# First layer's output product: two of four column chunks as groups of seven products of sums

## The chip, the cores and the metric

The kernel runs on one core of one Trainium2 chip. TensorE (PE) multiplies matrices, VectorE (DVE) and ScalarE (ACT) and GpSimd (POOL) work elementwise, SyncE (SP) issues most transfers. The time is device microseconds of one execution, the median of several. Engines run their own instruction queues in order and wait for one another by semaphores.

## The reference, cut to what matters

Two layers of a gated block over 16 meta tokens and 512 tokens (T = 528), width 1024, float32. What the change touches is the last line of the layer:

```python
def hybrid_layer(x, norm_g, w_in, qn_g, kn_g, pool_w, pool_b, pool_s, w_a, w_b, w_out, cos, sin, k_top):
    h = rms_norm(x, norm_g)
    proj = jnp.einsum('btd,de->bte', h, w_in)
    ...
    g_a, g_b = jnp.split(jax.nn.sigmoid(merge), 2, axis=-1)
    return x + jnp.einsum('btd,de->bte', g_a * y_a + g_b * y_b, w_out)
```

The second layer begins with the norm of this sum and its product with `w_in`.

## The kernel before

**Layout.** Activations stand with features on the partitions: `RES[0]` (the residual, 8 tiles of 128 features by 528 tokens), `hhi` and `hlo`. A float32 operand is split in a high part (a cast to a shorter format, on ACT) and a low part (what the cast left, by a subtraction on DVE or POOL); a product is then high x high + high x low + low x high, three matmuls for each 128 features. Tokens come in two halves, columns 0 to 272 and 272 to 528 (`halves`).

**Weights.** `chunks` (L116 to L135) lists column chunks of the weights in order of use: 256 columns of all 1024 rows of `w_out` make one. `w_load` (L158) fetches a chunk into two of four `raw` tiles (512 KB each) when the tiles of the chunk two before are free. `w_prep_enqueue` (L176) puts the steps that split it into the queue `prep_q`; `group_done` (L367) takes one step after each matmul group. There are three ways to split, each filling `w` tiles, of which there are eight:

- plain: two casts on ACT, two subtractions of 128x1024 on DVE (`high`, `low`), four `w` tiles.
- `by_dma`: ACT writes the negated high part into the low tile, then a transfer that POOL issues adds the raw weights to it in place (`minus`, L218), and ACT casts the high part (`plus`, L223). After `plus(1)` the raw tiles are given back once that transfer has landed, and POOL starts the first sum of the chunk behind (`first_sum`, L253).
- `mixed`: the four 512x128 blocks of a chunk become seven operands, each high and low: a12, a11, s2, s1, s3, s4, a22 (`mixed_prep`, L257, steps `i0` to `i8`). The sums s3 and s4 are made by transfers issued by POOL that add in place: `first_sum` (raw<-raw, L255) and raw<-s (L284); s2 and s1 by DVE. Each operand takes one `w` tile.

**Products of sums.** `group_of_products` (L992) multiplies a `mixed` chunk by seven sums of activations, in three PSUM banks U, S, X, with 12 matmuls a product in place of the eight blockwise products (Winograd's form): a11, a12, s2, s1, s3, s4, a22. Between products that add to one bank, ACT copies the bank out (`p1`, `u2`, `p5`), and DVE adds these parts (`total`) and hands the result on (`direct`). `prep_one` calls in it keep the split of the chunk behind going by a count (`base`, `LEAD`). Layer 0 uses it for the merging gates with 264 columns, layer 1 also for the last two chunks of its output (`mix_out`, L1146) with the sums of `sums_of_merged` (L1085) on 256 columns: `first` and `sums` make a0-a1, b1-a1 and -b1-a0, `lows` their low parts, `fourth`, `last_high`, `last_low` the fourth sum.

**Layer 0's output before.** All four chunks are plain. `out_group` (L1438) calls `dense` (L588): 24 matmuls into one bank, then DVE adds half of the bank to `RES[0]`, ACT squares the result, POOL adds the squares into `sq` (L1448). Chunks 0 and 1 run half by half; then chunks 2 and 3 are both ready and all of the first half runs before the second (loop at L1476), so that `stats(0)` (mean squares by one-column matmuls, then POOL's power) and `norm_half(1, 0, ...)` (scale by token, L503) of the first half run beside the four groups of the second half. Layer 1 begins with `plain_trio` (L571), which reads `nf`, the scaled first half, and raw weights for keys.

**Order of work.** PE's and DVE's queues are in the order written (`manual_schedule`); ACT's, POOL's and SP's are put in order when the program is built. `later(fn, n)` runs a step n groups later.

## Time and profile before

| | |
|---|---|
| median of three runs | 741.03 us (740.54 to 742.34) |
| the profiled execution | 740.78 us |
| its span, first to last instruction | 738.8 us |
| PE busy | 731.2 us (99%), 5949 matmuls |
| DVE busy | 590.0 us (80%) |
| ACT busy | 483.1 us (65%) |
| POOL busy | 246.1 us (33%) |
| layer 0's output product, first matmul to layer 1's first | 332.36 to 381.11 us |
| layer 1's groups of seven on its output | 709.6 to 731.6 us |

Rows in order of time read: start in us, length in us, engine, line, operation, tile written <- tiles read, sizes, count, and in brackets the idle time before and what ended it. A row "x3" is three instructions merged. Nearly all PE and DVE rows have line L63, the helper that records them, so they are told apart by tiles: `d` is a bank of a dense group, `a` a bank of small products, `w` split weights, `raw` fetched weights, `osum` the sums of the merged activations, `res` the residual, `sqs` the summed squares, `msq` the mean squares, `nf` the normed activations, `c`, `p`, `u` the parts inside a group of seven. In the stretches the number after each busy time is the count of instructions. DMA rows give the size and the median time from issue to landing.

### The profile page before, as it was taken

What the parts mean: (1) busy time and instruction counts of PE and PEld (TensorE: products, weight loads), DVE (VectorE), ACT (ScalarE), POOL (GpSimd) and SP (SyncE); (2) the same over time, 40 slices, a digit from 0 to 9 for tenths busy, and PEclk for the clock granted to TensorE, in tenths of its full rate; (3) what the DMA queues carried; (4) which work ended last, traced back from release to release, by engine and by line L of the source; (5) the groups of instructions that cost most, each with busy time, mean ns of one, the idle gap of its engine ahead of it and who ended that gap; (6) DMA issues with size and microseconds to landing.
All of it is one profiled execution on the core that took longest, in us unless ns stands there. A gap on an engine that the chain in (4) does not pass through costs nothing.

```text
span 738.8 us, 16099 instructions
## 1 busy us (share of the span) xinstructions
PE 731.2 (99%) x5949; PEld 705.3 (95%) x5949; DVE 590.0 (80%) x1500; ACT 483.1 (65%) x1099; POOL 246.1 (33%) x320
## 2 busy tenths in 40 slices
PE   8999999999999999999999999999999999999998
PEld 7999998899999999999999989998899999999997
DVE  6866999999997775894349668999989978768874
ACT  6769735656788886643245696367488978775643
POOL 3742173721222211163347421756031321106300
PEclk9999999999999999999999999999999999999999
DMA  8766765864564434543422678659565553439932
GB/s 266 232 171 157 165 153 115 217 157 101 134 126 114 93 81 114 173 160 116 144 89 86 171 170 201 158 125 204 114 148 110 142 115 89 116 104 266 203 88 72
DMA packets 103566, 106.41 MB, mean 144 GB/s; under 512 B 5008, under 2 KB 83632, under 8 KB 103488
## 3 DMA queue, kind: packets, MB, share of 16 engines
q1 hardware_dynamic: 91888, 74.89, 33.8%
q0 software_dynamic: 11520, 30.41, 22.9%
q8 instruction: 46, 0.75, 0.4%
q14 instruction: 32, 0.26, 0.1%
q10 hardware_dynamic: 80, 0.08, 0.1%
HBM read 66.41 MB, written 8.55 MB: 101 GB/s over the span
## 4 chain that ended last, share of the span: by engine, by line
PE 75%; DVE 17%; ACT 2%; DMA 2%; issue 2%; POOL 1%; SPq 1%; DVEq 0%; POOLq 0%; ACTq 0%
PE d L63 60%; PE a L63 10%; DVE sc L63 5%; PE v L63 4%; DVE m L63 3%; DMA xt<-in_x_dram 2%; DVE t L63 1%; DVE w L63 1%; DVE nf L63 1%; DVE silb L63 1%; DVE us L63 1%; DVE mlo L63 1%; DMA raw<-s 1%; ACT w L225 0%; SPq L156 0%
## 5 line engine op out<-in xcount | busy, mean ns | idle before, releaser
L63 PE MATMUL d<-hhi,w 128*128 128x256 f32 (+3 forms) x1392 | 278.4, 291 | 0.1
L63 PEld LDWEIGHTS d<-hhi,w 128*128 128x128 f32 x1392 | 222.2, 188 | 3.2 <-issue 0.6
L63 PE MATMUL d<-hlo,w 128*128 128x256 f32 (+3 forms) x696 | 189.8, 289 | 0.0
L63 PEld LDWEIGHTS d<-hlo,w 128*128 128x128 f32 x696 | 131.3, 189 | 1.4 <-issue 0.2
L63 DVE TENSOR_TENSOR w<-raw,w 128x512 fp32r<-128x512 f32 (+1 forms) x156 | 121.4, 784 | 13.3 <-ACT w L269 12.9
L63 PE MATMUL d<-hsum,w 128*128 128x264 f32 (+1 forms) x720 | 95.4, 285 | 0.1
L63 PEld LDWEIGHTS d<-hsum,w 128*128 128x128 f32 x720 | 89.5, 188 | 0.8 <-issue 0.3
L63 PE MATMUL d<-w,hhi 128*128 128x256 f32 x576 | 86.2, 287 | 0.7 <-ACT sq L668 0.7
L269 ACT CAST w<-raw 128x512 fp32r<-128x512 f32 x132 | 79.1, 623 | 5.6 <-DMA raw<-s 4.2
L63 PEld LDWEIGHTS d<-w,hhi 128*128 128x128 f32 x576 | 74.7, 188 | 5.2 <-issue 2.3
L255 POOL DMA_DIRECT2D raw<-raw x22 | 19.9, 903 | 114.2 <-DVE w L63 36.7
L221 POOL DMA_DIRECT2D w<-raw x34 | 31.5, 943 | 73.7 <-ACT w L220 51.1
L63 DVE MATCH_REPLACE8 sc<-m,sc 128x400 f32<-128x400 f32 (+2 forms) x100 | 54.3, 547 | 0.0
L63 DVE MAX8 m<-sc 128x8 f32<-128x400 f32 (+2 forms) x100 | 53.1, 555 | 0.9
L791 ACT ACTIVATE lt<-lt,mn,NR 128x144 f32<-128x144 f32 (+3 forms) x64 | 42.2, 661 | 12.1 <-DVE mn L63 12.0
L284 POOL DMA_DIRECT2D raw<-s x22 | 19.6, 892 | 90.6 <-DVE s L63 42.8
L63 DVE SCALAR_TENSOR_TENSOR sc<-r,wsg,sc 128x144 f32<-128x144 f32 (+3 forms) x56 | 32.4, 581 | 17.4 <-ACT r L714 15.0
L63 PE MATMUL d<-w,hlo 128*128 128x256 f32 x288 | 45.5, 281 | 0.0
L63 PE MATMUL d<-mhi,w 128*128 128x272 f32 (+2 forms) x192 | 45.3, 324 | 0.0
L806 POOL TENSOR_SCALAR pm<-lt,rs 128x16 f32<-128x16 f32 x48 | 27.9, 622 | 44.7 <-DVE rs L63 31.9
L677 POOL TENSOR_TENSOR t<-t,t 128x256 f32<-128x256 f32 (+1 forms) x34 | 32.5, 956 | 26.4 <-DVE t L63 25.0
L1420 POOL TENSOR_TENSOR hlo<-ta,hhi 128x256 fp32r<-128x256 f32 (+1 forms) x28 | 26.8, 968 | 41.5 <-PE d L63 29.4
(245 smaller groups left out, 1559.1 us busy)
## 6 DMA issues: line engine op xcount, KB each, us to landing
raw<-in_w_in_dram SPq DMA_DIRECT2D x88, 256.0 KB, 3.4
w<-raw POOLq DMA_DIRECT2D x34, 512.0 KB, 5.9
raw<-in_w_in_dram SPq DMA_DIRECT2D x32, 512.0 KB, 4.4
raw<-in_w_out_dram SPq DMA_DIRECT2D x12, 512.0 KB, 4.6
raw<-raw POOLq DMA_DIRECT2D x22, 256.0 KB, 4.0
raw<-s POOLq DMA_DIRECT2D x22, 256.0 KB, 3.7
kept<-res SPq DMA_DIRECT2D x16, 264.0 KB, 4.6
res<-kept SPq DMA_DIRECT2D x16, 264.0 KB, 6.3
```

Source lines behind the costliest of these rows:

```text
L63: return fn(*a, **k)
L221: gp.dma_start(t, raws[c][s], accum_op=OP.add)
L255: gp.dma_start(raws[c][0][:, 1], raws[c][0][:, 0], accum_op=OP.add)
L269: act.copy(t[:, 0], blk[src[n]])
L284: gp.dma_start(blk["a12"], blk["s2"], accum_op=OP.add)
L677: added[0] = gp.tensor_tensor(t1[:m, :256], t1[:m, :256], t2[:m, :256], op=OP.add).ins
L791: act.activation(L[hh][:, :n], L[hh][:, :n], AF.Exp, scale=NR[:, i, h:h + 1], bias=mn[:, hh:hh + 1], accum_out=sm[:, hh:hh + 1])
L806: (gp if j < 3 else dve).tensor_scalar(pms[i][:, 2 * j + hh, :], L[hh][:, 0:16], rs[:, hh:hh + 1], None, op0=OP.mult)
L1420: pool_end = gp.tensor_sub(hlo[:, j, a:a + n], d, f(hhi[:, j, a:a + n]))
```

## The change

Layer 0's output uses chunks 0, 1 (first token half), 2, 3, 1 again (second half) in this order. Chunks 0 and 1 are split `by_dma`, chunk 1 is fetched and split twice; chunks 2 and 3 are `mixed` and run as two groups of seven products on 264 columns. `sums_of_merged` takes the start and width of the halves; its sums lie in other tiles when the width is 264, and the low parts of the fourth sum go to POOL. They are made during chunks 0 and 1. `stats(0)` follows the first group of the last chunk; `norm_half(1, 0, ...)` is called in the middle of the last group, by the new argument `mid` of `dense`. The square sums of the first half need no separate last tile any more, which halves the matmuls of `stats(0)`. `more` in `group_of_products` takes up to four preparing steps earlier in the second group. `tight` names the mixed chunks that split a12 before a11.

```diff
         chunks += [[(w_rows(w_a[l], c, 512), 0)] for c in (0, 512)]
-        chunks += [[(w_rows(w_out[l], c, 256), 0)] for c in (0, 256, 512, 768)]
+        if l == 0:
+
+            by_dma |= {len(chunks), len(chunks) + 1, len(chunks) + 4}
+            mixed |= {len(chunks) + 2, len(chunks) + 3}
+            tight = {len(chunks) + 3}
+        chunks += [[(w_rows(w_out[l], c, 256), 0)] for c in (0, 256, 512, 768) + ((256,) if l == 0 else ())]
...
-        soon = c <= len(chunks) - 2
+        soon = c not in tight
...
-    def dense(w, mt_, a, n, rhs=H, kt=KT, late=False):
+    def dense(w, mt_, a, n, rhs=H, kt=KT, late=False, mid=None):
...
+            if mid and e + 1 == len(steps) // 2:
+                mid()
...
-            while prep_q and (popped[0] < base + 9 * r + LEAD + done[0] * 9 // 7 or (mid and done[0] > 4)):
+            while prep_q and (popped[0] < base + 9 * r + LEAD + done[0] * 9 // 7 + min(more * done[0], 4) or (mid and done[0] > 4)):
...
-    def sums_of_merged(ta):
+    def sums_of_merged(ta, s0, n2, lag):
 
-        c0, c1 = slice(16, 272), slice(272, 528)
-        t1 = one.tile([128, 2, 4, 256], F32R, tag="D", name="osum1")
+        c0, c1 = slice(s0, s0 + n2), slice(s0 + n2, s0 + 2 * n2)
+        t1 = one.tile([128, 2, 4, n2], F32R, tag="D", name="osum1")
...
+            both = one.tile([128, 2, 4, 2, n2], F32R, tag="C", name="osum23")
+            t2, t3 = ([both[:, w, k] for k in range(4)] for w in range(2))
...
-            dve.tensor_sub(t4[0][:, 1, k], ta[4 + k][:, c0], f(t4[0][:, 0, k]))
+            (dve if n2 == 256 else gp).tensor_sub(t4[0][:, 1, k], ta[4 + k][:, c0], f(t4[0][:, 0, k]))
...
-            for c in range(2):
-                w = chunk()
-                for mi in range(2):
-                    out_group(w, mi, 2 * c + mi, halves)
-            w2 = chunk()
-            flush_prep()
-            w3 = chunk(ahead=False)
-            for hs in (halves[:1], halves[1:]):
-                for c, w in ((2, w2), (3, w3)):
-                    for mi in range(2):
-                        out_group(w, mi, 2 * c + mi, hs)
-                    if c == 2 and hs[0][0] == 1:
-                        w_prep_enqueue()
-                if hs[0][0] == 0:
-                    later(lambda: stats(0), 1)
-                    later(lambda: norm_half(1, 0, mm, LAG2), 2)
+            w = chunk()
+            first, sums, lows, fourth, last_high, last_low, operands = sums_of_merged(ta, 0, T // 2, 4)
+            for k in range(4):
+                first(k)
+                sums(k)
+                later(lambda k=k: lows(k), 1)
+                out_group(w, k // 2, k // 2, k % 2)
+                if k < 2:
+                    prep_one()
+            w = chunk()
+            for mi in range(2):
+                out_group(w, mi, 2 + mi, 0)
+                prep_one()
+                prep_one()
+            later(lambda: [fourth(k) for k in range(4)], 1)
+            later(lambda: [last_high(k) for k in (0, 1)], 1)
+            later(lambda: [last_high(k) for k in (2, 3)], 2)
+            later(lambda: [last_low(k) for k in (0, 1)], 2)
+            later(lambda: [last_low(k) for k in (2, 3)], 3)
+            base, half = popped[0] - progress[W["use"]], T // 2
+            for q in range(2):
+                def direct(eh, t, src, q=q):
+                    grown(4 + 2 * q + eh, t * half, half, src, -0.5 if eh else 0.5)
+
+                def total(eh, t, ps, part, q=q):
+                    o = sheet(half, "c")[:, :half]
+                    dve.tensor_tensor(o, ps[:, :half], part, op=OP.add)
+                    direct(eh, t, o, q)
+
+                group_of_products(q, base, half, operands, total, direct, None, q)
+            w = chunk(ahead=False)
+            w_prep_enqueue()
+            out_group(w, 0, 2, 1)
+            stats(0)
+            out_group(w, 1, 3, 1, lambda: norm_half(1, 0, mm, LAG2))
             hooks = {0: lambda: stats(1), 1: lambda: norm_half(1, 1, mm, LAG3)}
```

58 lines of the change are left out of this document (32 added, 26 removed).

## The prediction

> **What bounds the kernel now.** I read the page, then the chain of waits (its pieces in order of time are used below), then busy times in four stretches of the span, then single rows in order of time around the change. The page's first line, and the stretches:
>
> ```profile
> span 738.8 us, 16099 instructions
> ```
> ```profile
> 332.40:350.10 17.70, 17.70 (x147) 17.59 (x146) 7.96 (x15) 6.40 (x11) 6.10 (x7) 1.00 0.37 121
> 350.10:368.10 18.00, 18.00 (x148) 18.00 (x147) 7.60 (x10) 4.57 (x8) 5.72 (x6) 1.00 0.49 147
> 368.10:381.10 13.00, 13.00 (x112) 12.69 (x111) 6.97 (x18) 5.62 (x12) 5.23 (x7) 1.00 0.11 42
> 709.60:731.60 22.00, 21.79 (x183) 21.33 (x182) 17.14 (x36) 11.98 (x28) 0.86 (x1) 1.00 0.20 49
> ```
>
> Columns of the stretches: length, then busy time of PE, PEld, DVE, ACT, POOL, then granted clock. The first three are the layer-0 output product: PE is never idle in 48.7 us, at clock 1.00, while DVE works 22.5 of them and ACT 16.6. TensorE alone sets the end here, so a matmul removed is a gain as long as nothing makes TensorE wait. The fourth stretch is layer 1's output, which already uses groups of seven products: there DVE is busy 17.1 of 22 us. The execution took 740.78 us (738.8 is its span, 2.0 lie around it); the runs' median is 741.03, 0.25 above.
>
> **Matmuls removed.** Call the first output matmul, 332.36, T.
>
> ```profile
> 332.36 0.29 PE L63 MATMUL d<-hhi,w 128*128 128x272 f32 x1
> ...
> 338.48 0.29 PE L63 MATMUL d<-hlo,w 128*128 128x272 f32 x1
> ...
> 341.48 0.28 PE L63 MATMUL d<-hlo,w 128*128 128x256 f32 x1
> ...
> 344.34 0.29 PE L63 MATMUL d<-hlo,w 128*128 128x272 f32 x1
> ```
> ```profile
> 370.90 0.20 PE L63 MATMUL a<-ones,sqs 128*16 128x1 f32 x2
> ...
> 372.00 0.36 PE L63 MATMUL d<-hhi,w 128*128 128x256 f32 x1
> ...
> 381.11 5.58 PE L63 MATMUL d<-raw,nf 128*128 128x200 f32 x32
> ```
> ```profile
> 223.83 4.38 PE d L63 x36
> ```
>
> The second rows of successive groups show 24 matmuls of 272 columns in 3.00 us (338.48 to 341.48) and of 256 in 2.86. The last row, from the chain, is three products of 12 at 264 columns in layer 0: 0.1217 us each, 1.46 a product. Four pairs of plain groups go, 4 x 5.86 = 23.44; fourteen products come, 168 x 0.1217 = 20.45: -3.0. The first half's statistics took 1.10 us (370.90 to 372.00) for six one-column matmuls; three remain, -0.55. Together -3.5 of the 48.75 from T to 381.11, if nothing waits.
>
> **Work added beside TensorE.** The two sevenfold chunks need 14 casts, 14 subtractions and 4 sums of 128x512 instead of four casts and four subtractions of 128x1024; the activations need 28 operations of DVE, 4 of POOL and 16 ACT casts at 264 columns, and 6 sums of DVE on the banks; the three plain chunks take their low parts by an accumulating transfer of POOL, with two ACT passes more each. The order of the changed program leaves each engine's queue strictly in line, so I follow the queues. Without waits six plain groups end at T+17.7, products P1 to P14 start there every 1.46 (P5 at 23.55, P8 at 27.95, P14 ends at 38.15).
>
> P1 costs nothing extra: its weights are split by DVE behind the fifth group's result (T+14.7): result and one low in 0.8, then low, sum, low at 0.6 apart (718.38 to 719.58 below holds two), done by T+17.5, needed at 17.95. The cover is 0.4; without it every 0.1 late is 0.1 on TensorE.
>
> **P5 waits for a copy behind a transfer (+0.9).** Before P5 adds to its bank, ACT must copy the half sum u out. In ACT's order that copy stands behind the casts of a chunk's last two blocks and four casts of the fourth sum, and the first of these casts waits for POOL's transfer raw<-s. POOL reaches that one only past the first sum of the *next* chunk, whose raw tile is free only when the plain chunk's accumulation has landed.
>
> ```profile
> 334.78 1.07 POOL L487 TENSOR_TENSOR Sg<-consts,gk 128x320 f32<-128x320 f32 x1
> ```
> ```profile
> 720.19 0.86 POOL L284 DMA_DIRECT2D raw<-s  x1 [13.40 <-DVE c L63]
> ```
> ```profile
> L1448 POOL TENSOR_TENSOR sqs<-sqs,tq x12: 736/773/1555, 342.6 to 381.9; 128x272 f32<-128x272 f32 x6, 128x256 f32<-128x256 f32 x6
> ```
> ```profile
> w<-raw POOLq DMA_DIRECT2D x34, 512.0 KB, 5.9
> ...
> raw<-in_w_out_dram SPq DMA_DIRECT2D x8, 256.0 KB, 4.2
> ```
> ```profile
> DMA to landing us min/median/max: 4.5/5.8/6.9
> ```
> ```profile
> DMA to landing us min/median/max: 3.7/4.1/4.5
> ```
> ```profile
> 710.65 0.74 ACT L1119 CAST osum<-ta 128x256 fp32r<-128x256 f32 x2 [3.26 <-DVE ta L63]
> 711.30 0.37 ACT L1019 COPY p<-d 128x256 f32<-128x256 f32 x1
> ...
> 712.08 1.14 ACT L269 CAST w<-raw 128x512 fp32r<-128x512 f32 x2
> 713.12 0.71 ACT L1119 CAST osum<-ta 128x256 fp32r<-128x256 f32 x2
> ```
>
> The first landing row is of w<-raw, the second of raw<-s, both in layer 1's end. POOL ends the tables at 335.85, plus one issue of 0.86 that now precedes them: T+4.35. The accumulation lands 5.9 later (10.25), the next chunk's load takes 4.2 (14.45), its first sum 0.86 (15.3), three adds of squares 0.77 each (17.6), raw<-s lands 4.1 later (21.7). Then ACT: two casts 1.05 (712.08 to 713.12), two pairs at 0.65 (710.65 to 711.30), the copy 0.4: 24.45 against 23.55. Bounds: with landings of 4.5 and 3.7 nothing; with 6.9 and 4.5 and adds of 1.56, the longest in the rows, 0.9 + 1.0 + 0.4 + 2.4 = 4.7. I take 0.9, the medians.
>
> **P8 waits for DVE (+0.5).** The next chunk's first block is split in DVE's queue behind P5's and P6's results. Layer 1 shows the same rows at the same product:
>
> ```profile
> 717.58 0.42 DVE L63 TENSOR_TENSOR c<-d,p 128x256 f32<-128x256 f32 x1
> ...
> 718.38 0.68 DVE L63 TENSOR_TENSOR w<-raw,w 128x512 fp32r<-128x512 f32 x1
> ...
> 719.58 0.42 DVE L63 TENSOR_TENSOR c<-d,u 128x256 f32<-128x256 f32 x1
> ...
> 720.38 0.68 DVE L63 TENSOR_TENSOR w<-raw,w 128x512 fp32r<-128x512 f32 x1
> ```
> ```profile
> 718.85 1.67 PE L63 MATMUL d<-osum,w 128*128 128x256 f32 x12
> 720.60 0.41 PE L63 MATMUL a<-consts,res 128*128 128x128 f32 x2
> ...
> 721.11 0.50 PE L63 MATMUL d<-hhi,w 128*128 128x256 f32 x2
> ```
>
> From 717.58 to the end of the low at 721.06 are 3.5 us, 0.2 after P5's end; P8's third matmul is due 2.92 + 0.25 after it, so it waits 0.5. In layer 1 the third matmul came at 721.11, where 12 x 0.119 after 718.85, a transpose pair of 0.14 and two matmuls give 720.65: 0.45 was lost. Bounds 0.3 to 1.1 (one collision of the kind below).
>
> **Last plain chunk (+1.05).** Its second accumulation is issued at the end of a chain from P5: P5's total on DVE (0.25 + 0.45 + 0.43), squares on ACT (0.5), the add on POOL (0.8), raw<-s (4.1), two casts (1.05), first negated cast (0.95), u (0.4), second negated cast (1.0), squares (0.5), add (0.75), landing 5.9: 17.1 after P5's end. The group that needs it reaches its 21st matmul after nine products (13.15), P8's 0.5 and 20 x 0.119 = 2.4: 16.05. The same chain passes P12's copy u at 8.95, due at 9.25: free, 0.3 to spare. Bounds for the group: 0 (landings 3.7 and 4.5) to 2.9 (4.5, 6.9, slower adds).
>
> **End of the layer.** The first half's norm had four groups as cover and now has half a group.
>
> ```profile
> 372.17 0.21 DVE L63 TENSOR_SCALAR msq<-a 16x1 f32<-16x1 f32 x2 [0.74 <-PE a L63]
> ...
> 375.63 1.72 DVE L63 SCALAR_TENSOR_TENSOR nf<-res,parT,a 128x272 f32<-128x272 f32 x4
> ```
> ```profile
> 372.46 0.88 POOL L495 TENSOR_TENSOR msq<-msq,mhalf 128x3 f32<-128x3 f32 x1 [5.43 <-DVE msq L63]
> ```
>
> From the last statistics matmul (372.00) to the ready scale (373.34) are 1.35 us; twelve matmuls cover 1.43. I take 0, bounds 0 to 0.4. The scaled tiles then come faster than layer 1 reads them: four in 1.72, the rest and four lows in some 3.5 more, while TensorE still has 1.43 to go and takes 5.58/8 = 0.7 per tile.
>
> ```profile
> raw<-in_w_in_dram SPq DMA_DIRECT2D x88, 256.0 KB, 3.4
> ```
> ```profile
> 660.03 28.39 PE d L63 x240
> ```
>
> Layer 1's key weights load only after the first negated cast's accumulation (about 14.5 after P5's end), take 3.4 and are wanted at 21.3: 3 to spare. On SP the stores of two finished result tiles stand ahead of layer 1's first load; they wait for P7's result (T+29), the load for its raw tile till T+32 anyway. The early plain chunks' double ACT passes and POOL transfers lie under layer 0's merging product; layer 1 has them at the same place, and the chain's last row shows 240 matmuls there without a break. Cost 0; uncovered, a late weight would cost its own lateness.
>
> Sum: -3.5 + 0.9 + 0.5 + 1.05 = -1.05: 739.7 for this execution, **740.0** as a median.
>
> **A rule weighed.** For transfers issued by POOL the Trainium skill (DMA: Bandwidth & Descriptors, Anatomy of one DMA) gives about 2.0 us plus bytes over 436 GB/s, an estimate of 3.2 us for 512 KB. By it the waits of P5 and of the last chunk vanish and the sum is -3.0. The row has 5.9 over 34 transfers and the sum goes by that.
>
> **The rivals.**
>
> *Transfers land early.* If the accumulations land at their quickest (4.5, 3.7), P5 and the last chunk wait for nothing and only P8's 0.5 stays: -3.0, 738.0. For it: in the first two stretches the transfer engines are 0.37 and 0.49 busy. Against: 5.9 is the median of 34, and 4.5 the quickest of the four in the landing row.
>
> *DVE and POOL hold each other up.*
>
> ```profile
> 330.82 2.52 POOL L1420 TENSOR_TENSOR hlo<-ta,hhi 128x272 fp32r<-128x272 f32 x2 [0.89 <-ACT hhi L1418]
> ```
> ```profile
> 330.94 1.80 DVE L63 TENSOR_TENSOR w<-raw,w 128x1024 fp32r<-128x1024 f32 x1
> ...
> 341.93 1.22 DVE L63 TENSOR_TENSOR w<-raw,w 128x1024 fp32r<-128x1024 f32 x1
> ```
>
> The first subtraction of DVE ran beside POOL's, the second without one: 0.58 more. POOL's four new subtractions fall in the time of P5 to P7, where DVE's queue feeds P8; two collisions there are 1.2 more: 741.2. The Trainium skill (SBUF — State Buffer, Who interferes with whom) says that a DVE operation with two SBUF inputs and a reading GpSimd operation take turns whole; the pair of rows agrees.
>
> *POOL's queue is the bound, and it is slower.* The next chunk's first sum sits in POOL's queue ahead of this chunk's raw<-s. If the landings and adds take their upper bounds, P5 waits 4.7 instead of 0.9: 743.8. It decides from the point where raw<-s lands after T+22.75 (P5's wait of 1.95 eats the gain); beyond 24.95 it is slower by 0.3%. For it: three transfers in series before one cast, and DVE, which slows POOL's adds, is to do some 37 of 45 us (22.5, less eight 1024-wide lows at 1.22, plus 18 operations at 0.6 and 34 at 0.4). Against: it needs all of them late at once.
>
> **Numbers.** 0.3% (2.2 us) is about what a measurement can tell from no change. Forecast 740.0, its own spread 739.0 to 741.0: 0.46. Early landings, 738.0: 0.30. Collisions, 741.2: 0.11. POOL's queue, 743.8: 0.13. Below 738.8 lies nearly all of the second and a little of the first: 0.31 faster. Above 743.2 lies most of the last: 0.11 slower; same 0.58. The range takes in the early landings and reaches two thirds of the way to the last: 737.9 to 742.6.
>
> **What would show it.** Right: products at 1.46 us, a TensorE gap of about 1 us before P5 ended by ACT's copy, 0.5 at P8's third matmul ended by DVE, 1 us at the 21st matmul of the last chunk's first group ended by a transfer, and none before layer 1's first matmul. Wrong: TensorE waits at the norm's transposes or at layer 1's start, gaps in groups that I call free, or raw<-s landing far from T+21.7.

## The result, and the profile after

The changed kernel takes 749.73 us (median of four, 748.93 to 751.33), the kernel before 740.83 beside it: ratio 1.0119 with a 95% interval of 1.0096 to 1.0141. Slower by 8.9 us, where 740.0 was forecast. First line of the page, then TensorE's rows of the section in order of time, those with an idle time in front, and the first row of layer 1:

```profile
span 749.6 us, 16186 instructions
```
```profile
336.70 0.39 PE L63 MATMUL d<-hlo,w 128*128 128x272 f32 x1 [0.67 <-DVE hlo L63]
...
351.89 0.28 PE L63 MATMUL d<-hlo,w 128*128 128x264 f32 x1
353.88 0.51 PE L63 MATMUL d<-hhi,w 128*128 128x264 f32 x2 [1.71 <-DVE w L63]
...
360.75 1.73 PE L63 MATMUL d<-osum,w 128*128 128x264 f32 x12 [0.98 <-ACT u L1027]
...
367.45 0.51 PE L63 MATMUL d<-hhi,w 128*128 128x264 f32 x2 [1.78 <-DVE w L63]
...
380.77 0.74 PE L63 MATMUL d<-hhi,w 128*128 128x256 f32 x4 [1.19 <-DMA w<-raw]
383.29 0.74 PE L63 MATMUL d<-hhi,w 128*128 128x256 f32 x4 [1.79 <-DMA w<-raw]
...
390.98 5.58 PE L63 MATMUL d<-raw,nf 128*128 128x200 f32 x32
```

Six waits: in the first plain group, at the third matmul of product 1, before product 5, at the third matmul of product 8, and twice in the last chunk's first group. They add up to 8.12 us. Before, the section had none. Each costs a little more than its bracket: the matmul behind 351.89 was due 0.12 later, at 352.01, and came at 353.88, 1.87 late for 1.71 of idle time, since the idle time counts from the end of the draining matmul. Six times 0.16 is about 1.0.

The stretches after the waits (length; busy time of PE, PEld, DVE, ACT, POOL with counts; granted clock; DMA share, GB/s):

```profile
380.00:384.00 4.00, 1.44 (x9) 1.11 (x10) 0.00 (x0) 0.00 (x0) 0.00 (x0) 1.00 0.74 176
384.00:388.00 4.00, 4.00 (x20) 3.74 (x19) 0.64 (x3) 0.42 (x1) 1.58 (x2) 0.50 0.98 308
388.00:392.00 4.00, 4.00 (x22) 3.98 (x22) 3.25 (x8) 1.90 (x5) 1.64 (x2) 0.64 0.11 40
392.00:396.00 4.00, 4.00 (x25) 4.00 (x25) 3.77 (x8) 2.66 (x6) 1.63 (x2) 1.00 0.19 67
```

The third number from the end is the granted clock: 0.50 and 0.64 for eight microseconds in which TensorE is busy throughout. That is 4 x 0.50 + 4 x 0.36 = 3.4 us lost without one idle time to show it. The balance: -3.5 of matmuls, +8.1 of waits, +1.0 behind them, +3.4 of clock gives +9.0. The section, from the first output matmul (333.11) to layer 1's first (390.98), takes 57.87 us against 48.75, +9.12. The profiled execution is the slowest of the four, 1.6 us above their median. Its span is 10.8 us longer than before: 9.12 in the section, 0.93 behind it and 0.75 ahead of it, where two executions of the same code differ as much (first output matmul at 332.36 before, at 333.45 in a run below that changes layer 1 alone).

Who is busy while the waits at 1, 5 and 8 arise:

```profile
350.00:372.00 22.00, 17.52 (x139) 16.89 (x138) 21.24 (x35) 12.06 (x27) 11.83 (x13) 1.00 0.39 110
```

DVE, 21.2 of 22 us. TensorE is no longer what sets the pace here. Part of the 21.2 is DVE's own work and part is operations made longer beside POOL; a run below tells them apart. DVE's rows and, below them, POOL's:

```profile
334.00 2.64 DVE L63 TENSOR_TENSOR hlo<-ta,hhi 128x272 fp32r<-128x272 f32 x1 [1.20 <-ACT hhi L1430]
...
346.15 2.24 DVE L63 TENSOR_TENSOR ta<-ta 128x264 f32<-128x264 f32 x2
...
362.62 0.43 DVE L63 TENSOR_TENSOR c<-d,p 128x264 f32<-128x264 f32 x1 [0.59 <-PE d L63]
...
363.58 1.25 DVE L63 TENSOR_TENSOR w<-raw,w 128x512 fp32r<-128x512 f32 x1
364.75 1.23 DVE L63 TENSOR_TENSOR s<-raw 128x512 f32<-128x512 f32 x1
...
366.71 0.69 DVE L63 TENSOR_TENSOR w<-raw,w 128x512 fp32r<-128x512 f32 x1
```
```profile
333.71 0.89 POOL L261 DMA_DIRECT2D raw<-raw  x1
334.36 1.16 POOL L492 TENSOR_TENSOR Cg<-consts,gk 128x320 f32<-128x320 f32 x1
335.20 1.14 POOL L493 TENSOR_TENSOR Sg<-consts,gk 128x320 f32<-128x320 f32 x1
...
347.00 1.09 POOL L1458 TENSOR_TENSOR sqs<-sqs,tq 128x272 f32<-128x272 f32 x1
...
363.32 2.11 POOL L1458 TENSOR_TENSOR sqs<-sqs,tq 128x264 f32<-128x264 f32 x2
```

A 128x512 operation takes 0.69 us alone (366.71) and 1.25 or 1.23 beside additions of squares (363.58, 364.75). The 272-wide subtraction at 334.00, which takes 1.01 in a run below and 0.44 in another, ends only when both tables are through (335.20 + 1.14). The chain of waits, last, on the transfer of the last two waits:

```profile
374.14 0.68 POOL sqs L1458
374.83 8.42 DMA w<-raw
383.25 0.04 issue
```

8.42 us where the median of 34 was 5.9; the transfer issued before it, at 372.73, took 8.0 and ends the first of the two waits. Both fly beside layer 1's first loads, with the transfer engines at a share of 1.08 from 376 to 380 us (0.17 there before). That the loads are what makes them long is argued from this; no run takes the loads away.

### The profile page after: what moved, and what is told of

Read it like the earlier page. It is cut to its first block, busy times and chain, and to the rows that moved or that the text cites. A ratio compares the mean times of both kernels' runs of the same rounds, so it can differ in the third digit from the quotient of the medians.

```text
span 749.6 us, 16186 instructions
## 1 busy us (share of the span) xinstructions
PE 732.1 (98%) x5919; PEld 704.8 (94%) x5919; DVE 611.4 (82%) x1544; ACT 501.4 (67%) x1139; POOL 255.7 (34%) x335
## 4 chain that ended last, share of the span: by engine, by line
PE 69%; DVE 17%; DMA 4%; ACT 3%; issue 3%; POOL 2%; SPq 1%; DVEq 0%; POOLq 0%; ACTq 0%
PE d L63 55%; PE a L63 10%; PE v L63 4%; DVE sc L63 3%; DVE m L63 2%; DVE w L63 2%; DMA xt<-in_x_dram 2%; DMA raw<-s 2%; DVE t L63 1%; DMA w<-raw 1%; DVE ta L63 1%; POOL us L1352 1%; DVE s L63 1%; DVE us L63 1%; DVE mlo L63 1%
## 5 line engine op out<-in xcount | busy, mean ns | idle before, releaser
L63 PE MATMUL d<-hhi,w 128*128 128x256 f32 (+3 forms) x1312 | 267.3, 294 | 7.0 <-DVE w L63 3.9
L63 PEld LDWEIGHTS d<-hhi,w 128*128 128x128 f32 x1312 | 211.9, 190 | 11.2 <-DVE w L63 5.0
L63 PE MATMUL d<-hlo,w 128*128 128x256 f32 (+3 forms) x656 | 182.0, 290 | 0.7 <-DVE hlo L63 0.7
L63 PEld LDWEIGHTS d<-hlo,w 128*128 128x128 f32 x656 | 124.8, 190 | 2.1 <-DVE hlo L63 0.9
L275 ACT CAST w<-raw 128x512 fp32r<-128x512 f32 x144 | 86.4, 623 | 13.0 <-DMA raw<-s 10.0
L261 POOL DMA_DIRECT2D raw<-raw x24 | 21.6, 901 | 124.0 <-DMA raw<-in_w_in_dram 15.7
L227 POOL DMA_DIRECT2D w<-raw x40 | 36.8, 950 | 77.4 <-ACT w L226 53.1
L290 POOL DMA_DIRECT2D raw<-s x24 | 21.2, 884 | 91.0 <-DVE s L63 47.3
L226 ACT ACTIVATE w<-raw 128x1024 fp32r<-128x1024 f32 x40 | 41.8, 1058 | 4.0 <-PE d L63 4.0
L231 ACT CAST w<-raw 128x1024 fp32r<-128x1024 f32 x40 | 41.5, 1054 | 0.0
```

Source lines behind the costliest of these rows:

```text
L63: return fn(*a, **k)
L226: act.activation(t, raws[c][s], AF.Copy, scale=-1.0)
L227: gp.dma_start(t, raws[c][s], accum_op=OP.add)
L231: act.copy(t, raws[c][s])
L261: gp.dma_start(raws[c][0][:, 1], raws[c][0][:, 0], accum_op=OP.add)
L275: act.copy(t[:, 0], blk[src[n]])
```

## The experiments

Section is the time from the first output matmul to layer 1's first, rest from there to the end of the span, both in the profiled execution. The columns 1, 5 and 8 are the waits at these products, and a dash is no wait. The kernel before took 740.4 to 741.5 as a median beside them; the ratios go by its runs on the same chip.

| kernel | first group | 1 | 5 | 8 | later | section | rest | median | ratio to the kernel before |
|---|---|---|---|---|---|---|---|---|---|
| before | - | | | | - | 48.75 | 357.69 | 740.83 | 1 |
| after | 0.67 | 1.71 | 0.98 | 1.78 | 1.19, 1.79 | 57.87 | 358.62 | 749.73 | 1.0119 |
| last chunk by DVE | 0.67 | 1.70 | 1.34 | 1.17 | - | 51.46 | 358.90 | 744.42 | 1.0042 |
| all plain chunks by DVE | - | 3.74 | - | 1.24 | - | 52.70 | 359.85 | 747.56 | 1.0081 |
| without POOL's elementwise work | 0.55 | - | 1.36 | 0.50 | 0.89, 1.83 | 54.57 | 358.86 | 747.31 | 1.0082 |
| before, two chunks by transfer | - | | | | - | 48.60 | 358.19 | 740.86 | 0.9997 |
| tables early | - | 0.85 | 0.62 | 1.60 | - | 49.78 | 358.50 | 744.43 | 1.0042 |
| additions held, first try | - | - | 1.19 | 1.41 | 0.44 | 49.49 | 358.83 | 743.53 | 1.0030 |
| before, artificial waits | - | | | | 2.53, 5.21, 2.62, 2.61 | 70.20 | 358.07 | 761.92 | 1.0275 |
| planner's values restored | - | 0.85 | 0.84 | 1.96 | - | 51.11 | 357.39 | 742.14 | 1.0022 |
| additions behind raw<-s | - | - | 0.62 | 3.46 | - | 51.31 | 357.35 | 744.27 | 1.0047 |
| before, with after's order in layer 1 | - | | | | - | 48.77 | 360.18 | 743.90 | 1.0040 |
| seven additions after 369 us | - | - | 0.53 | 0.81 | 3.44 | 53.12 | 357.42 | 745.61 | 1.0059 |
| four additions after 371 us | - | 1.03 | 1.61 | 0.54 | 0.96 | 50.17 | 357.38 | 742.35 | 1.0020 |
| few additions | - | - | 0.28 | 1.09 | - | 48.43 | 357.32 | 740.90 | 0.9999 |
| copy first | - | - | - | 1.28 | - | 48.28 | 357.36 | 740.65 | 0.9991 |
| high parts first | - | - | - | 0.46 | 0.35 | 48.28 | 357.37 | 740.68 | 0.9999 |

### The last chunk's low parts by DVE

```diff
-            by_dma |= {len(chunks), len(chunks) + 1, len(chunks) + 4}
+            by_dma |= {len(chunks), len(chunks) + 1}
```

> The changed kernel, with the last plain chunk's low parts made by DVE instead of the accumulating transfers. In the changed kernel's trace the last group lost 3.0 us to two waits for these transfers, and the 48 matmuls after them ran at a granted clock of 0.50 to 0.64 and lost about 3.6 us more. Theory: the transfers are the cause of the waits, and the waits of the lower clock, since DVE is nearly idle from 373 to 378 us. Then both go: 749.7 - 3.0 - 3.6 = 743 us, granted clock 1.00 to the end of the layer. Rival 1: the lower clock follows from all the earlier waits or from the end of the layer as such; then only the 3.0 go, 746.7. Rival 2: the two 128x1024 subtractions are late as well (each 1.22 us): the waits stay above 1 us and end by DVE, 746 or more.

Measured 744.42, interval of the ratio 1.0026 to 1.0058. The last two waits are gone and the clock stays up, in the stretches of the same columns:

```profile
380.00:384.00 4.00, 4.00 (x34) 3.69 (x33) 0.65 (x4) 0.42 (x1) 1.79 (x3) 1.00 0.55 197
384.00:388.00 4.00, 4.00 (x29) 4.00 (x28) 4.00 (x10) 2.47 (x6) 1.74 (x3) 1.00 0.00 0
```

The theory holds, to 1.4 us: the transfers made the waits, and with them the clock's fall goes. The last group's statistics, transposes and layer 1's start now run without a wait and at full clock, so the short cover of the first half's norm, which the forecast costed at nothing, did cost nothing.

### All three plain chunks by DVE

```diff
-            by_dma |= {len(chunks), len(chunks) + 1, len(chunks) + 4}
...
             if s == 1:
                 del raws[c]
                 w_load()
+                first_sum(c + 1)
...
-            prep_q.extend((lambda: high(0), second, lambda: low(1)))
+            prep_q.extend((lambda: high(0), second, lambda: low(1)) + ((lambda: None,) if c + 1 in mixed or c + 2 in mixed else ()))
```

> The changed kernel, with the low parts of all three plain chunks made by DVE. Beside what the run with the last one alone shows, it moves four 128x1024 subtractions (1.22 to 1.80 us each) onto DVE around the first output matmul. Theory that DVE's own load before the first product sets its wait: the wait at the fifth group of matmuls of the first output group (0.7) goes, and the wait at the first product grows from 1.7 by about 2.4, as at least two of the four subtractions fall behind the activation sums: about 0.8 to 2 us slower than the run with the last chunk alone. Rival: the four subtractions fit ahead of the output product, as in the kernel before; then it is 0.8 faster than that run.

747.56 (1.0052 to 1.0111, two executions), 3.1 above the last run, whose interval it just touches. Product 1's wait grew from 1.70 to 3.74, by 2.0 where the theory had about 2.4, and the first group's went. The edit also moves the first sum of the chunk behind: POOL issues it behind the tables here (at 336.29), and DVE's subtraction of the merged activations takes 1.00. What the theory had not: that one wait brought the clock down by itself.

```profile
354.89 0.51 PE L63 MATMUL d<-hhi,w 128*128 128x264 f32 x2 [3.74 <-DVE w L63]
```
```profile
355.00:358.50 3.50, 3.50 (x20) 3.50 (x21) 3.50 (x7) 1.74 (x4) 1.72 (x2) 0.63 0.46 78
```

So the transfers of the two early chunks are worth their place: they take four 128x1024 subtractions off a DVE that is full.

### Without POOL's elementwise work

```diff
-                    gp.tensor_tensor(sq[:, a:a + n], sq[:, a:a + n], t[:, :n], op=OP.add)
...
-            (dve if n2 == 256 else gp).tensor_sub(t4[0][:, 1, k], ta[4 + k][:, c0], f(t4[0][:, 0, k]))
+            if n2 == 256:
+                dve.tensor_sub(t4[0][:, 1, k], ta[4 + k][:, c0], f(t4[0][:, 0, k]))
+            else:
+                act.copy(t4[0][:, 1, k], ta[4 + k][:, c0])
```

> The changed kernel without POOL's elementwise work in the output product: the eleven additions of squares are left out, and the fourth sum's low parts are written by ACT (a copy of the sum, so the values are not the reference's) instead of subtracted by POOL. Theory: POOL's operations hold DVE up (in the changed kernel's trace a 128x512 operation of DVE takes 1.24 us beside them, 0.68 alone), and DVE's lateness makes the waits at products 1 and 8. Then those two waits (1.7 and 1.8 us) fall under 0.5 each, and the last chunk's transfers start about 1 us earlier: 749.7 - 2.8 - 1 = about 746, or about 742 if the clock then stays up. Rival: DVE is late by its own work; then each of the two waits stays above 1.2 us and the time above 748.

747.31 (1.0041 to 1.0123). The tables stay. Product 1 waits for nothing, although the tables hold the subtraction of the merged activations up as before (2.52 us). Product 8 waits 0.50, the 0.5 of the forecast. DVE's rows up to product 8's weights:

```profile
359.83 0.43 DVE L63 TENSOR_TENSOR c<-d,p 128x264 f32<-128x264 f32 x1 [2.42 <-PE d L63]
...
360.64 0.69 DVE L63 TENSOR_TENSOR w<-raw,w 128x512 fp32r<-128x512 f32 x1
361.25 0.69 DVE L63 TENSOR_TENSOR s<-raw 128x512 f32<-128x512 f32 x1
...
362.66 0.68 DVE L63 TENSOR_TENSOR w<-raw,w 128x512 fp32r<-128x512 f32 x1
```

From the first row to the end of the last are 3.51 us, the 3.5 of the forecast; in the changed kernel they were 4.78 (362.62 to 367.40), and the two operations in the middle took 1.25 and 1.23. DVE over the same 22 us, counted from the section's start:

```profile
348.90:370.90 22.00, 20.14 (x162) 19.71 (x162) 16.95 (x35) 15.80 (x35) 3.41 (x4) 1.00 0.49 129
```

It is busy 17.0 us instead of 21.2, in as many operations. POOL's work beside DVE is the cause of what products 1 and 8 wait for beyond the forecast. The waits for the transfers and the low clock after them stayed (0.89 and 1.83), which is why the time is no lower. Product 5's 1.36 is in part this run's own: two of the copies that ACT makes in POOL's place stand ahead of u and take 0.6.

### The kernel before, with the first two chunks by transfer

```diff
+        if l == 0:
+            by_dma |= {len(chunks), len(chunks) + 1}
         chunks += [[(w_rows(w_out[l], c, 256), 0)] for c in (0, 256, 512, 768)]
```

> The kernel before, with one part of the change: the low parts of the first two output chunks by accumulating transfers. Theory: the transfers' issues on POOL beside the tables hold DVE's last subtraction of the merged activations up, so the first output group waits 0.7 us as in the changed kernel: 740.8 + 0.7 = 741.5. Rival 1: that wait needs the first sum of the next sevenfold chunk, which is not there; then no wait, 740.8 or a little less as DVE has four subtractions fewer. Rival 2: the transfers themselves land too late for the plain groups: waits ended by a transfer, 742 or more.

740.86 (0.9986 to 1.0008): no wait, TensorE busy without a break, and the subtraction of the merged activations in 1.01 us.

```profile
333.10:381.70 48.60, 48.60 (x401) 48.29 (x400) 19.10 (x38) 18.45 (x33) 17.53 (x22) 1.00 0.46 129
```
```profile
334.01 1.01 DVE L63 TENSOR_TENSOR hlo<-ta,hhi 128x272 fp32r<-128x272 f32 x1 [1.20 <-ACT hhi L1420]
```

The first rival holds: the wait of the first group needs the sevenfold chunk's first sum, whose issue (333.71, 0.89 us) pushes the tables from 333.84 to 334.36. Here the subtraction is through after the first table, in the changed kernel only after both. The run with all plain chunks by DVE agrees: with the first sum behind the tables it has no such wait. The early transfers themselves cost nothing, as the forecast said.

### Layer 1's tables early

```diff
+        if l == 0:
+            tables(1, True)
         for c in range(2):
             w = chunk()
...
-            with tc.issue_after(pool_end.ins):
-                tables(1, True)
```

This stands on the run with the last chunk by DVE.

> The run with the last chunk's low parts by DVE, and layer 1's tables Cg and Sg made before the merging product, where POOL is idle, instead of between the last output activations and the plain chunks' transfers. Theory: POOL's tables and the first sum of the sevenfold chunk held DVE's subtraction up (2.64 us for a 128x272 operation, 0.42 alone); DVE works without a gap from there to product 8, so its 1.6 us late are what product 1 waits for too. Then the wait in the first output group goes (0.7 to 0) and product 1's falls from 1.7 to about 0.3; with the copy before product 5 earlier as well, the time falls by about 2.2 to 2.5 from 744.4, to 742. Rival: the 512-wide block operations beside additions of squares set product 1's wait; then only the 0.7 go, 743.7.

In the profiled execution the first group waits for nothing, product 1's wait is halved (0.85, where 0.3 was expected), product 5's as well, and the section is 1.7 us shorter, although product 8's wait grew from 1.17 to 1.60. DVE's subtraction, and POOL beside it:

```profile
334.22 0.44 DVE L63 TENSOR_TENSOR hlo<-ta,hhi 128x272 fp32r<-128x272 f32 x1 [1.20 <-ACT hhi L1432]
```
```profile
334.18 2.12 POOL L227 DMA_DIRECT2D w<-raw  x2
```

Two transfer issues of POOL on top of the subtraction, and it takes 0.44: these two issues did not hold DVE up, the tables did. The Trainium skill (SBUF — State Buffer, Who interferes with whom) has it that a DVE operation with two SBUF inputs contends with a GpSimd instruction that reads SBUF, with whole instructions taking turns; this pair of rows and the 2.64 of the changed kernel agree. The median, 744.43 (743.43 to 745.14, the profiled one being the lowest), did not fall though. The clock does not explain it: over a whole execution it was 1.00 in three of the four and 0.997 in one (744.60). With four and five executions, and a part ahead of the section that varies by more than 1 us, a gain of 1.7 in one profiled section is not shown as a gain of time.

### Additions of squares held back, first try

```diff
+                    keep = (j, a) in ((1, 0), (1, HB), (2, 0)) or j in (4, 5)
...
+                    held.append(add) if keep else add()
...
                 def direct(eh, t, src, q=q):
+                    if q:
+                        while held:
+                            held.pop(0)()
```

> The same, and seven of POOL's additions of squares (of the first two plain groups, of the third and of the first four products) held back until product 10, when DVE has no block operations left; their squares lie in a tile that is free then. Theory: these additions lengthen DVE's 512-wide operations by 0.55 each; without them the waits at products 1 and 8 fall under 0.3 and 0.6, the output product then saves what its 3.5 us of matmuls are worth less about 1.5: 739.5, faster than the kernel before by a little over 1. Rival 1: the held additions, at 0.76 each, end after the last plain group and delay the statistics by 1 us or more: 741 or more. Rival 2: POOL's subtractions of the fourth sum do the same harm alone, product 8 still waits 1 us: 740.5.

743.53 (1.0020 to 1.0041), where 739.5 was expected. POOL's queue is put in order when the program is built, and the additions went back between the same operations, at 348.0, 354.6 and 362.4 us. Product 1's wait went; for product 8 the run says nothing.

### Artificial waits in the kernel before

```diff
...
+            def stall(n):
+                z = tmp.tile([128, HB], F32R, tag="tt", name="zz", bufs=6)[:, :256]
+                for i in range(n):
+                    act.copy(z, f(z) if i else seen_banks[-1][:, :256])
+                pe.matmul(bank("a")[:, :16], z[:, :128], z[:, :16], start=True, stop=True)
...
```

> The kernel before with artificial waits of TensorE: a matmul that reads the end of a chain of ACT copies of the bank just filled. One chain of four copies after the second output group pair, one of ten after the fourth, and two of four, one plain group apart, after the last two groups of the first half. Estimated from the rows of ACT copies (0.33 apart, 0.4 at the ends): waits of 1.7, 3.7, 1.7 and 1.7 us. Theory: one wait of about 3 us or more within some 4 us brings the granted clock down to 0.5 for the next 5 to 7 us and costs about 3 us beyond itself, and a wait of 1.7 does not: the clock falls once, after the long chain; the time is 741.5 + 8.8 + 3 = 753. Rival 1: the clock follows the sum of the waits in the whole section or the end of the layer; it falls only after the last chains or not at all, 750. Rival 2: any wait brings it down; it falls after each, over 758.

761.92 (1.0229 to 1.0321, two executions), where 753 was expected. The waits came out longer than estimated, 2.53, 5.21, 2.62 and 2.61 us, and the clock fell after every one of them. Stretches, by wait and by what follows it:

```profile
345.20:348.00 2.80, 0.27 (x3) 0.20 (x2) 0.42 (x1) 1.89 (x5) 0.73 (x1) 1.00 0.81 279
348.00:351.40 3.40, 3.40 (x16) 3.40 (x16) 0.00 (x0) 0.00 (x0) 0.00 (x0) 0.50 0.00 0
351.40:361.40 10.00, 10.00 (x82) 9.80 (x81) 3.57 (x5) 3.71 (x6) 3.06 (x3) 1.00 0.26 83
361.40:366.60 5.20, 0.00 (x0) 0.00 (x0) 3.23 (x3) 4.87 (x12) 1.07 (x1) 0.85 0.91 273
366.60:371.90 5.30, 5.29 (x23) 5.29 (x24) 0.00 (x0) 0.00 (x0) 0.00 (x0) 0.50 0.27 77
371.90:378.30 6.40, 6.40 (x52) 6.27 (x50) 0.88 (x2) 0.87 (x2) 1.54 (x2) 1.00 0.00 0
```

After the first, 3.4 us at 0.50 and then full clock; after the second, 5.3 us. The waits are 12.9 us in all and the stretches at low clock cost some 7.7 more; the section took 70.2, 21.5 more than before. The theory's threshold of 3 us was too high: 2.5 us are enough. Rival 1 falls: nothing of the layer's end is needed. Rival 2, that any wait is enough, has its time here, but this run has no short wait to try it; the changed kernel has, and its 1.71 and 1.78 at products 1 and 8 left the clock at 1.00. The Trainium skill (TensorE: Matmul & The Clock Gate, Part 1) describes a gate that halves the clock after an idle window of some 3.4 us and opens after a busy one of that length. The half and the 3.4 us to come back are here; the idle time needed is shorter than that by a quarter at least.

### The planner's values restored

```diff
+            credit[0], spare[0] = 0.1, 1.8
             hooks = {0: lambda: stats(1), 1: lambda: norm_half(1, 1, mm, LAG3)}
```

> The run with the tables made early, and at the end of layer 0 the planner's two running values (the credit that places small steps between matmul groups, 0.9 after the changed output product and 0.1 after the old one, and the spare DVE time, -0.73 and 1.8) set to what the kernel before has there, so that layer 1 gets the order of the kernel before on every engine. From layer 1's first matmul to the end the kernel before took 357.7 us, the run with the tables early 358.5, the changed kernel 358.6. Theory: this order is what costs 0.8 to 0.9 us outside the output product; then 357.7 to 358.1 here and a time 0.5 to 0.9 below the run before it, with the section unchanged. Rival: the length of the program or the state of the buffers costs it; then 358.5 again.

The rest fell from 358.50 to 357.39, the level of all later runs of the changed kernel (357.32 to 357.42); the ratio from 1.0042 to 1.0022 (742.14, 1.0012 to 1.0031), which is 1.5 us. The theory holds, and by a little more than its 0.9. The section rose in this execution: product 8 waited 1.96 and the clock then stood at 0.50 from about 367.1 to 370.5. That is no mark of the kernel: over a whole execution the clock was 0.998 in two of the ten, the profiled one (743.35) and one of 743.57, and 0.999 or 1.00 in the others.

### The kernel before, with the changed kernel's order in layer 1

```diff
+            credit[0], spare[0] = 0.9, -0.73
             hooks = {0: lambda: stats(1), 1: lambda: norm_half(1, 1, mm, LAG3)}
```

> The kernel before, with the planner's two values at the end of layer 0 set to those of the changed kernel (credit 0.9, spare -0.73): layer 0 is as before, layer 1 has the changed kernel's order. Theory: that order alone costs 0.8 to 0.9 us from layer 1's first matmul to the end, 358.6 instead of 357.7 to 358.2, and as much in the time, 742.2. Rival: the order costs nothing by itself, 357.7 to 358.2 and 741.4.

743.90 (1.0025 to 1.0055). Section 48.77, untouched; rest 360.18. Two numbers that the scheduler of the program carries over, and that nobody edited, cost 2 to 2.5 us here, where 0.8 to 0.9 was expected, and about 1 in the changed kernel.

### Additions behind the transfer raw<-s

```diff
...
+                            with tc.issue_after(moved[0].ins):
+                                held.pop(0)()
```

> The same, and seven of POOL's additions of squares held back, this time queued on POOL behind the second transfer raw<-s (in the earlier run with held additions the scheduler put them at their old places: 348.0, 354.6, 362.4 us). Theory: DVE is in work without a gap from 338 to 372 us, so each of its operations lengthened beside POOL delays product 8's weights one for one; without six of these collisions (0.55 us each and more) product 8's wait falls from 1.6 to 0.5 or less, product 5's from 0.6 to 0.3, product 1's from 0.85 to 0.3; the section then takes 48.75 - 3.5 + 1.1 + 0.4 for the refilling of TensorE behind waits = 46.8 and the time is about 1.5 below the kernel before. Rival: DVE's own work is too much for the time up to product 8 (37 us in 45); then product 8 waits over 1 us and the time is no less than the kernel before.

Product 1's wait went and product 8's rose to 3.46; 744.27 (1.0032 to 1.0062). DVE's row, and POOL's:

```profile
363.21 3.42 DVE L63 TENSOR_TENSOR w<-raw,w 128x512 fp32r<-128x512 f32 x1
```
```profile
363.63 7.08 POOL L1466 TENSOR_TENSOR sqs<-sqs,sqt 128x272 f32<-128x272 f32 x7
```

Seven additions stand back to back, and one subtraction of 0.69 us takes 3.42 among the first of them. It says nothing for the rival, since DVE's own work was not the cause, but it shows how far a row of POOL operations can hold one of DVE.

### Additions after the last block operation of DVE

```diff
-                            with tc.issue_after(moved[0].ins):
+                            with tc.issue_after(added_sq[0].ins):
...
-                    keep = (j, a) in ((1, 0), (1, HB), (2, 0)) or j in (4, 5)
+                    keep = j in (4, 5)
```

The edit is shown against the run before it. The last two lines belong to the second of two runs alone.

> The run with the tables early and the planner's values restored, and the same seven additions of squares queued on POOL behind the first addition of the second sevenfold chunk (at about 373 us), when DVE has no block operation left. In the last run with held additions seven of them stood back to back from 363.6 us and one 128x512 subtraction of DVE took 3.42 us among them. Theory: freed of both, DVE comes to product 8 about 1.2 us earlier than with the additions in their old places: waits at product 1 none, at 5 about 0.6, at 8 about 0.7, no fall of the granted clock; against that eleven additions in a row from 373 us end after the last plain chunk's first group, about 1 us late for the statistics. Section 47.5 to 48.5, the rest 357.4: about 1 to 2 us below the kernel before, 739.5 in a run where the kernel before takes 740.8. Rival: DVE's own work decides product 8; it waits 1.5 or more, the clock falls again, and the time is above the kernel before.

> The same with only the four additions of the first sevenfold chunk's results queued there; the other three stay at 346 to 350 us. Theory: product 8's wait falls from 1.96 to about 0.8 (two 512-wide operations at 0.68 instead of 1.25), no fall of the clock and no late statistics, while product 1's 0.85 and product 5's 0.84 stay: section 48.75 - 3.5 + 2.5 + 0.4 = 48.2, 0.5 to 1 us below the kernel before. Rival as above.

Product 8 came to 0.81 and 0.54. Both theories hold there, and both fail at the statistics, which wait for POOL:

```profile
379.68 1.15 PE L63 MATMUL a<-ones,sqs 128*16 128x1 f32 x6 [3.44 <-POOL sqs L1466]
```

That row is of the run with seven; its wait cost the clock as well (0.50 from 379.7 to 384.5), 745.61 (1.0042 to 1.0076). With four the wait is 0.96, product 1 keeps 1.03 and product 5 has 1.61, which the expectation did not foresee: the transfer raw<-s, which the casts ahead of u wait for, took 5.1 us to land, 4.3 in the run with the planner's values restored; 742.35 (1.0011 to 1.0030).

### Few additions

```diff
...
+                    for row in () if hf else (0, 1):
+                        pe.matmul(sp[:m, t:t + 1], sqt[0][:, row, s:s + m], ones, start=False, stop=row == 1)
...
+                    elif j > 3 or a:
+                        held.append(add)
```

> The run with the tables early and the planner's values restored; of POOL's additions of squares, the two of result tiles 1 and 2 (first half) are not made, TensorE sums their squares in the statistics instead (six one-column matmuls more, 0.1 each), and three more (of the first group's second half and two results of the first sevenfold chunk) are queued behind the first addition of the second sevenfold chunk. Theory: no addition stands beside DVE's work for products 1 and 8, and only three additions are late, so the statistics do not wait: product 1 no wait, product 5 about 0.5, product 8 about 0.8, statistics 0 and 0.6 longer; section 48.75 - 3.5 + 1.3 + 0.6 + 0.3 = 47.5, the rest 357.4: 1.5 below the kernel before, granted clock 1.00 throughout. Rival: DVE's own work sets product 8 (over 1.2 us), or the statistics still wait for POOL (over 1 us): the time is not below the kernel before.

740.90 (0.9989 to 1.0008): the whole loss made good, nothing gained. No wait at product 1 or at the statistics, 0.28 at product 5, 1.09 at product 8 (expected 0.8), the section 48.43 instead of 47.5.

### The copy first

```diff
-            later(lambda: [last_high(k) for k in (2, 3)], 2)
+            later(lambda: behind(last_high, 2, 3), 3)
...
-            later(lambda: [last_low(k) for k in (2, 3)], 3)
+            later(lambda: [last_low(k) for k in (2, 3)], 4)
+            def behind(fn, *ks):
+                with marked():
+                    for k in ks:
+                        fn(k)
```

> The same, and two of the fourth sum's four casts on ACT queued behind the copy u instead of ahead of it (their subtractions on POOL one product later). Theory: product 5 waits for the place of u in ACT's queue, two casts at 0.33 ahead of it gone take 0.65 off, so its wait falls from about 0.5 to 0, and the time by 0.3 to 0.5 from the run before it. Rival 1: the transfer raw<-s, which two casts still ahead of u wait for, sets it; then the wait stays. Rival 2: product 7 or 8 waits longer, as the fourth sum's low parts come later; nothing gained.

Product 5 waits for nothing. ACT's rows:

```profile
355.80 0.72 ACT L1131 CAST osum<-ta 128x264 fp32r<-128x264 f32 x2
356.43 0.37 ACT L1027 COPY u<-d 128x264 f32<-128x264 f32 x1
356.70 0.72 ACT L1131 CAST osum<-ta 128x264 fp32r<-128x264 f32 x2
```

The casts ahead of u were what was left of that wait; the transfer is not late once DVE is not: it lands at T + 21.6, where the forecast had T + 21.7. Product 8 has 1.28 instead of 1.09 (the second rival, in part), the section 0.15 less: 740.65, ratio 0.9991 (0.9983 to 1.0000). It is the best of these kernels, and still no gain that could be told from none.

### High parts first in products 1 and 8

```diff
+            steps = [(k, x, y) for k in range(4) for x, y in ((0, 0), (0, 1), (1, 0))]
+            if more is not None and name == "a11":
+                steps.sort(key=lambda s: s[1])
...
```

> The run with the copy first, and in products 1 and 8 the eight matmuls with high weights run ahead of the four with low weights. Theory: product 8 waits for its own low part only, which is then needed 0.73 us later (six matmuls at 0.122): the wait falls from 1.28 to about 0.55 and the section from 48.28 to 47.55, about 1.2 below the section of the kernel before with the rest 0.3 below: about 739.6 where the kernel before takes 741.0. Rival: DVE's queue as a whole is late; product 9 or 10 then waits for what product 8 no longer does, and the section stays at 48.2 or more.

The rival holds for the time, though not at the products it named: the wait at product 8 fell by 0.8 and the section stayed at 48.28 to the hundredth.

```profile
363.83 0.88 PE L63 MATMUL d<-hhi,w 128*128 128x264 f32 x5 [0.46 <-DVE w L63]
...
365.87 4.94 PE L63 MATMUL d<-osum,w 128*128 128x264 f32 x36
370.65 0.36 PE L63 MATMUL d<-hhi,w 128*128 128x264 f32 x1
...
372.71 1.73 PE L63 MATMUL d<-osum,w 128*128 128x264 f32 x12 [0.35 <-DVE c L63]
```

0.35 of it turns up at product 14, ended by DVE. The 36 matmuls of products 10 to 12 from 365.87 take 4.78 us to the next row, where 36 x 0.1217 is 4.38; the weights of product 12 have a wait there, ended by ACT's copy u:

```profile
369.08 1.52 PEld L63 LDWEIGHTS d<-osum,w 128*128 128x128 f32 x12 [0.30 <-ACT u L1028]
```

So what product 8 no longer waits for, later products wait for, one behind DVE and one behind ACT. Median 740.68, ratio 0.9999 (0.9991 to 1.0008).

## Why the prediction was wrong

The section was forecast at -1.05 and came at +9.12. Of the 10.2 us between them, collisions of DVE and POOL make 3.7, the last chunk's transfers 1.9 more than was priced, the refilling of TensorE behind its waits 1.0 and the lower clock 3.4.

*Matmuls removed, -3.5:* right. Products follow each other at 1.46 wherever nothing waits (36 matmuls from 370.21 to 374.61 in the changed kernel, 4.40).

*"P1 costs nothing extra ... The cover is 0.4":* the step that failed first. The wait was 1.71. The sum took DVE's operations at their durations alone; in truth POOL's operations beside them make them longer, and since DVE works nearly without a gap from about 338 us (32.3 of 34 us to 372), what lengthens an operation is paid at the next product. Without POOL's additions and subtractions product 1 waited for nothing, as forecast, although the tables were as late; with the tables early and POOL's other work left, 0.85 remained. The additions are thus the larger part, and the tables add to what they leave. The 37 of 45 us of DVE work stood in the text, but as an argument for a rival, and as an average; over the 22 us that matter DVE was busy 21.2, of which 17.0 were left without POOL's work.

*P8, +0.5, bounds 0.3 to 1.1:* measured 1.78. The 0.5 is what product 8 waits for without POOL's work (0.50 in that run, with DVE's rows 3.51 us long), so the mechanism was right, and the missing term is collisions. "DVE and POOL hold each other up" was a rival at 0.11 with two collisions at product 8, 1.2 us. There were some at every stage: in the first group, at product 1 and at product 8, 3.7 us beyond the forecast (0.67 + 1.71 + 1.78 - 0.5). What was read off the pair of rows at 330.94 was not carried through POOL's list of operations.

*P5, +0.9:* 0.98, right in size by luck, wrong in cause. The transfer raw<-s left at 353.53 because DVE's sum was late, not because POOL's queue was: it landed at T + 24.9 instead of T + 21.7. TensorE had waited itself and was 2.9 us late by then, so that nearly the same wait was left. With DVE in time, two casts ahead of the copy are left.

*Last plain chunk, +1.05, bounds 0 to 2.9:* mis-sized. 2.98 of waits: the chain was 1.2 us longer than forecast (issue at 374.83, 12.4 after product 5's end, not 11.2) and the transfer took 8.42, beyond the 6.9 that was the longest row; the first accumulation, which the sum did not price, took 8.0 and made a wait of its own, 1.19. The bound came from a stretch where the transfer engines had room (a share of 0.20); here layer 1's loads fly beside it (1.08).

*Not in the sum at all:* the clock, +3.4, shown by the run without the last transfers, by the run whose one wait of 3.74 did the same, and by the artificial waits; refilling TensorE behind six waits, +1.0; and layer 1's order, about +0.9, shown by restoring two values in the one kernel and by setting them in the other. The forecast took the rest of the program as given. The 1.0 is worked out from the rows; no run isolates it.

*Costed at nothing:* right for the early transfers and for the norm's cover and layer 1's start. Wrong for the first plain group, 0.67, through the first sum's place in POOL's queue ahead of the tables.

*The weighed rule* of the Trainium skill (DMA: Bandwidth & Descriptors, Anatomy of one DMA; 3.2 us for such a transfer as an estimate) would have been further off: 5.7 is the median after, 8.42 the one that decided.

What stays open: why the transfer raw<-s took 5.1 us in the run with four additions late; whether layer 1's loads make the last chunk's transfers long; and about half a microsecond of the section in the last three runs: with the copy first, 48.75 - 3.0 for the matmuls + 0.5 for the longer statistics (1.60 instead of 1.10) + 1.4 for the one wait gives 47.65 of the 48.28.

## What to carry to other kernels

Before matmuls are traded for elementwise work, add up the helping engine's work in the very window between first need and last need, with each operation at the length it has beside its neighbour's: DVE's own work was 17.0 of 22 us, and collisions made it 21.2. Price a TensorE wait with what follows it: from about 2 us on, it cost half its followers' clock for 3 to 7 us more in these runs. And where a program plans its own order, an edit reaches everything behind it; compare the order of the untouched part before blaming the touched one.

## What the runs showed of the hardware

The clock's fall hangs on the wait and not on the work: single waits up to 1.78 us left it at 1.00, those of 1.96, 2.53, 2.61, 2.62, 3.44, 3.46, 3.74 and 5.21 brought it down, and so did two of 1.19 and 1.79 half a microsecond of matmuls apart, and two of 0.89 and 1.83. Low stretches lasted from 3.4 to some 7 us.

One DVE subtraction waited through several POOL additions in a row: 3.42 us for 0.69. Two transfer issues of POOL at the same moment did not lengthen one (0.44).
